# Two slot rings of an encoder trunk kernel: token-major evictions and Strassen weight loads drawn from other rings

## The chip, the cores and the metric

The kernel runs on one core of one Trainium2 chip. The metric is the device time of one execution in microseconds (us); lower is better. A time given for a kernel is the median of several executions; the profile and its trace come from one execution of their own. Engines are called by the profile's names: PE (matrix engine; PEld its weight loads), DVE (vector), ACT (scalar), POOL (GpSimd) and SP, whose queue issues nearly all DMAs.

## The reference

One layer (DEPTH is 1) over 512 tokens and 2048 channels, all float32. A conditioning vector gives six modulation vectors. A normed and modulated copy of x goes through one input projection whose columns feed four token mixers; their outputs are concatenated and projected back; then comes a gated convolutional feed-forward network of width 5504.

```
mod = cond @ ada_w[l] + ada_b[l]
h = rms_norm(x, mix_pre_g[l]) * (1.0 + sc_m) + sh_m
y = token_mixers(h, w_in[l], ...)            # DeltaNet | chunked attn | sliding window | gMLP, then @ w_out
x = x + gt_m * rms_norm(y, mix_post_g[l])
h = rms_norm(x, ffn_pre_g[l]) * (1.0 + sc_f) + sh_f
a, gt = split(h @ w_up, 2)
y = (gelu(causal_dwconv(a, conv_w) + conv_b) * gt) @ w_down
x = x + gt_f * rms_norm(y, ffn_post_g[l])
```

## The kernel before

**Matmuls.** Every large product is made from float32 operands that are split into a high and a low part; three matmuls of 128x128 by 128x512 stand for one. The split of a weight tile is one ACT copy (hi) and one DVE subtraction (lo); where it is "shadowed", ACT first copies the tile to PSUM as well (sh), and DVE subtracts that.

**Stages.** First the modulation vectors and the first input-projection groups ("early"), then the DeltaNet mixer with its long chain of small steps. The remaining ("late") input-projection groups bv, bk, ck, dv, bq, cq, du are written in the code after that chain, but the compiler that orders the queues mixes them into it: it lets each engine take what is ready, earlier lines of the code first. So PE fills the chain's pauses with late matmuls. Then come the other mixers, the output projection, and the feed-forward network. In that, three of 43 feature tiles are computed plainly (`up_plain`, PLAIN), the other 40 by a Strassen scheme: 20 blocks of the up projection (two passes `p` of ten) and 10 blocks of the down projection.

**Rings.** A tile with a tag takes one of the tag's `bufs` slots; a slot comes free when all readers of its former tile are done, and the slots of one tag go out in the order of the code. The rings that matter here:

- "t" in pool `tp`: NT_ = 3 slots of 128x512. It serves, among others, the evictions of the late groups: `ev_late_tm` (L762, token-major groups bv and dv, four evictions `lt` each, PSUM to SBUF by ACT, then a DMA to the DRAM buffer `std`) and `ev_late_fm` (`lf`).
- "xn" in pool `gp`: NBR = 5 slots. It holds the normed x while the early groups run; `rtile` draws from it for `bg_row`, `gate_row` and `ff_row`, whose rows are used from the output projection on.
- Three rings of four 128x1024 slots each for Strassen weights: `wraw` (pool `wp`, also the ring of all earlier weight loads, that of `up_plain` too), "raw1" (pool `ap`) and "raw2" (pool `dn`). `draw()` goes through them in a fixed order of twelve. A block (`fast_block`, L1449) draws eight, two for each of four j.

**The change of stage.** The activations h2 of the feed-forward network lie in pool `hp` as 16 hi and 16 lo tiles of 2 KB per partition (hl0 to hl15, then hh0 to hh15), 64 KB on the right-hand side. After the plain tiles `hold.close()` gives them up, and `dn` is opened there with waits tile by tile: its 46 KB (five t2, two ar, three hi and three lo, four raw2) lie on the last 46 KB of those 64, that is from hl9 on, with its tags in the order in which the code first asks for them: before, t2, ar, hi, lo, raw2. Just ahead of that, `late_sums` uses the four slots of "raw1" to load h2 blocks, form sums on DVE and store them to `h2d`.

**A block** has seven steps of 24 matmuls (X and Z are its PSUM banks). Step i needs A[i] (`a_tile`: load `ar`, hi on ACT, lo on DVE for even i and on POOL for odd) and one quarter of every weight pair; POOL makes the combined quarters T1 to T4 (L1468, L1471, L1473, L1475), of which T2 goes to a t2 tile and is used in step 2. In block 0, A[0] and A[1] are loaded ahead and A[2] to A[6] after steps 0 to 4.

**The tail.** After the last block, `wraw()` loads six units of plain down weights, and ten further `draw()` calls load gate rows and residual rows.

Of the kernel before, what the change touches and what calls it, by code (L numbers as in the profile page):

```python
# [10 lines left out]
F32 = mybir.dt.float32  # L11
# [5 lines left out]
P = 128  # L17
# [8 lines left out]
UW = 1024  # L26
# [223 lines left out]
def trunk_kernel(ctx: ExitStack, tc: tile.TileContext, a: dict, out: bass.AP):  # L250
# [26 lines left out]
    def nm(s):  # L277
        uid[0] += 1
        return f"{s}{uid[0]}"

    def mt(s="m", shape=(P, 512), dt=F32):
        return cur[0].tile(list(shape), dt, tag="m", name=nm(s))

    def tt_(s="t"):
        return tp.tile([P, 512], F32, tag="t", name=nm(s))
# [76 lines left out]
    def wraw():  # L362
        return wp.tile([P, UW], F32, tag="raw", name=nm("raw"), bufs=NRAW)
# [293 lines left out]
    for s, ks in enumerate(KSTEPS):  # L657
# [6 lines left out]
        for i, g in enumerate(gs):  # L664
# [6 lines left out]
            n = -(-len(fs) // max(1, len(gs) - 2 - i)) if s else FS0[i]  # L671
# [22 lines left out]
    def rtile(s, dt=F32):  # L694
        if mixing_open[0]:
            return gp.tile([P, 512], dt, tag="xn", name=nm(s), bufs=NBR)
        return mt(s, dt=dt)
# [62 lines left out]
        nc.sync.dma_start(out=std[STG[n_] + j], in_=t)  # L760

    def ev_late_tm(key, tt, ps, step):  # L762
        t = tt_("lt")
        S.activation(t, ps, AF.Gelu_apprx_tanh if key == "dv" else AF.Copy)  # L764
        nc.sync.dma_start(out=std[STG[key] + tt], in_=t)

    def late_groups(name, rate):
        pace[0] = rate
        for g in late:
            if (g[1][0][0] if g[0] == "FM" else g[1]) == name:  # L770
                if g[0] == "FM":
                    fm_group(g, ev_late_fm)
                else:
                    tm_group(g, ev_late_tm)

    def staged(name, j):
        t = mt("sd")
        nc.sync.dma_start(out=t, in_=std[STG[name] + j])
        return t
# [83 lines left out]
    for tt in range(NTT):  # L863
# [4 lines left out]
        t = mt("kp")  # L868
# [4 lines left out]
    for tt in range(NTT):  # L873
# [3 lines left out]
        t = mt("vt")  # L877
# [64 lines left out]
    for j in range(31):  # L942
        n = 31 - j
# [130 lines left out]
    for tt in range(NTT):  # L1074
        t = staged("dv", tt)
# [5 lines left out]
    for tt in range(NTT):  # L1081
        t = tmt[("dv", tt)]
        V.tensor_scalar(t, t, mv[:, tt, 0:1], vr[:, tt:tt + 1], ALU.subtract, ALU.mult)
        V.tensor_tensor(t, t, sgg, ALU.mult)
    for g in range(4):
# [4 lines left out]
        t = cur[0].tile([P, 512], F32, tag="sgo", name=nm("sgo"), bufs=4)  # L1090
# [7 lines left out]
    for h in range(H):  # L1098
# [18 lines left out]
        for j in range(NTT):  # L1117
# [3 lines left out]
            t = mt("pt")  # L1121
# [18 lines left out]
    for h in range(H):  # L1140
# [21 lines left out]
        for i0 in (0, 2):  # L1162
# [6 lines left out]
            t = mt("ct")  # L1169
# [235 lines left out]
    dn = [None]  # L1405
# [15 lines left out]
    def draw():  # L1421
        n = nraw[0] % (NRAW + NRAW1 + NRAW2)
        nraw[0] += 1
        if NRAW1 <= n < NRAW + NRAW1:
            return wraw()
        if n < NRAW1:
            return ap_[0].tile([P, UW], F32, tag="raw1", name=nm("raw"), bufs=NRAW1)
        return dn[0].tile([P, UW], F32, tag="raw2", name=nm("raw"), bufs=NRAW2)

    def t2(dt=F32):  # L1430
        return dn[0].tile([P, 512], dt, tag="t2", name=nm("t2"), bufs=NP + 1)
# [18 lines left out]
    def fast_block(A, src, units, bank, evict, after, own=False):  # L1450
        b = []
        for j in range(NP):
            d = {}
            for x, (k0, k1) in enumerate((("B11", "B12"), ("B22", "B21"))):
                raw = draw()
                nc.sync.dma_start(out=raw, in_=src[units[2 * j + x]])
                d[k0], d[k1] = raw[:, 0:512], raw[:, 512:]
            b.append(d)
# [153 lines left out]
    for ui, (uk, uc) in gdn[0]:  # L1612
        raw = wraw()
# [7 lines left out]
    for c in (0, 2):  # L1621
        t = draw()
        nc.sync.dma_start(out=t, in_=gtd[c:c + 2, :].rearrange("c n -> (c n)").partition_broadcast(P))
        gts.append(t)
    for tt in range(NTT):
        sl = slice(tt * P, (tt + 1) * P)
        sq = st(4)
        x1 = []
        for h in range(2):
            t = draw()  # L1630
            nc.sync.dma_start(out=t, in_=x1d[tt, h])
            x1.append(t)
        for cb in range(4):
            ps = mx("dl")
            for f in PLAIN:
                ah, al = acts[f]
                wh, wl = ws[(f, cb)]
                tm_mm(ps, ah[:, sl], al[:, sl], wh, wl, f == PLAIN[0], f == PLAIN[-1])
            y = ya[tt][cb]
            V.tensor_tensor(y, y, ps, ALU.add)  # L1640
            S.activation(t2(), y, AF.Square, accum_out=sq[:, cb:cb + 1])  # L1641
            G.tensor_tensor(y, y, gts[cb // 2][:, cb % 2 * 512:(cb % 2 + 1) * 512], ALU.mult)
        ss = st(1)
        V.reduce_sum(ss, sq, AX.X)
        r, _ = rstd(ss, D, "rf")
        for cb in range(4):
            y = ya[tt][cb]
            V.scalar_tensor_tensor(y, y, r, x1[cb // 2][:, cb % 2 * 512:(cb % 2 + 1) * 512], ALU.mult, ALU.add)  # L1648
            nc.sync.dma_start(out=out[sl, cb * 512:(cb + 1) * 512], in_=y)
# [6 lines left out]
NRAW = 4  # L1656
NHL = 5
NRAW1 = 4
NRAW2 = 4
# [29 lines left out]
```

## Time and profile before

| | |
|---|---|
| median of 3 runs | 2326.6 us (2317.59 to 2331.16) |
| profiled execution, its own time | 2319.29 us, of which the span is 2316.8 us |
| mean granted TensorE clock | 0.979 of full speed |
| PE busy | 2189.0 us, 94% of the span |
| DVE, ACT, POOL busy | 73%, 63%, 46% |
| DMA | 480.24 MB, mean 207 GB/s |

PE is busy in all but about 128 us of the span. Busy shares are averages over stages with different limits, so what a change in one place is worth is read from the idle time of PE in that place, and from what ended it. In the timeline a bracket behind an instruction gives the time for which its engine was idle before it, and the instruction or DMA that ended this wait.

### The profile page before, as it was taken

What the parts mean: (1) busy time and instruction counts of PE and PEld (TensorE: products, weight loads), DVE (VectorE), ACT (ScalarE), POOL (GpSimd) and SP (SyncE); (2) the same over time, 40 slices, a digit from 0 to 9 for tenths busy, and PEclk for the clock granted to TensorE, in tenths of its full rate; (3) what the DMA queues carried; (4) which work ended last, traced back from release to release, by engine and by line L of the source; (5) the groups of instructions that cost most, each with busy time, mean ns of one, the idle gap of its engine ahead of it and who ended that gap; (6) DMA issues with size and microseconds to landing.
All of it is one profiled execution on the core that took longest, in us unless ns stands there. A gap on an engine that the chain in (4) does not pass through costs nothing. (4 is left out here: it accounts for less than half of the span.)

```text
span 2316.8 us, 31339 instructions
## 1 busy us (share of the span) xinstructions
PE 2189.0 (94%) x9852; PEld 1734.0 (75%) x9852; DVE 1680.9 (73%) x2665; ACT 1463.4 (63%) x2638; POOL 1077.0 (46%) x848
## 2 busy tenths in 40 slices
PE   5999999989999998989999999999999999999998
PEld 3878876767677786767788887777777777877776
DVE  5887678877878545956665568788788767777777
ACT  5767465355567544666777677776776677666663
POOL 4663032243323200256445465755765765564643
PEclk8999999999999999999999999999999999999999
DMA  8876555677888754678853547456545634435333
GB/s 299 285 259 236 170 183 180 198 240 254 295 306 284 248 171 146 231 257 291 282 206 137 182 167 273 160 198 213 190 176 204 216 141 173 155 106 194 119 132 137
DMA packets 206574, 480.24 MB, mean 207 GB/s; under 512 B 32692, under 2 KB 74180, under 8 KB 206408
## 3 DMA queue, kind: packets, MB, share of 16 engines
q1 hardware_dynamic: 199576, 477.19, 59.1%
q10 hardware_dynamic: 6832, 1.06, 0.2%
q8 instruction: 78, 1.28, 0.2%
q14 instruction: 88, 0.72, 0.1%
HBM read 399.50 MB, written 78.67 MB: 206 GB/s over the span
## 5 line engine op out<-in xcount | busy, mean ns | idle before, releaser
L1481 PE MATMUL X<-hi,ah 128*128 128x512 f32 x960 | 386.8, 403 | 19.3 <-DVE c L1493 6.1
L435 POOL TENSOR_TENSOR ga<-ga,ada 128x512 f32<-128x512 f32 (+1 forms) x167 | 226.5, 1356 | 369.5 <-ACT ada L434 348.9
L1482 PE MATMUL X<-lo,ah 128*128 128x512 f32 x960 | 383.7, 400 | 1.0 <-DVE lo L1447 1.0
L1483 PE MATMUL X<-hi,al 128*128 128x512 f32 x960 | 383.4, 399 | 0.0
L1447 DVE TENSOR_TENSOR lo<-raw,hi 128x512 fp32r<-128x512 f32 x360 | 264.2, 764 | 110.7 <-ACT hi L1446 110.2
L1468 POOL TENSOR_TENSOR raw<-raw 128x512 f32<-128x512 f32 x120 | 161.9, 1353 | 319.3 <-ACT hi L1443 232.1
L1481 PE MATMUL Z<-hi,ah 128*128 128x512 f32 x720 | 286.8, 398 | 6.4 <-ACT c L1491 2.9
L1444 DVE TENSOR_TENSOR lo<-raw,sh 128x512 fp32r<-128x512 f32 x360 | 240.1, 683 | 72.2 <-ACT sh L1442 35.6
L1442 ACT ACTIVATE sh<-raw 128x512 fp32r<-128x512 f32 x360 | 210.5, 588 | 124.1 <-DMA raw<-w_dn 63.3
L1483 PE MATMUL Z<-hi,al 128*128 128x512 f32 x720 | 285.7, 397 | 0.8 <-POOL al L1418 0.8
L1482 PE MATMUL Z<-lo,ah 128*128 128x512 f32 x720 | 285.4, 396 | 0.0
L1446 ACT ACTIVATE hi<-raw 128x512 fp32r<-128x512 f32 x360 | 214.4, 625 | 95.2 <-PE X L1483 36.4
L1443 ACT ACTIVATE hi<-raw 128x512 fp32r<-128x512 f32 x360 | 221.4, 622 | 35.7 <-PE Z L1483 24.9
L1481 PEld LDWEIGHTS X<-hi,ah 128*128 128x128 f32 x960 | 183.1, 191 | 66.5 <-DVE c L1493 7.4
L380 PE MATMUL acc<-hh,hi 128*128 128x512 f32 x544 | 221.3, 410 | 9.2 <-ACT lt L764 6.7
L382 PE MATMUL acc<-hh,lo 128*128 128x512 f32 x544 | 221.5, 410 | 4.2 <-DVE lo L374 4.1
L381 PE MATMUL acc<-hl,hi 128*128 128x512 f32 x544 | 222.4, 409 | 0.4 <-POOL hl L493 0.3
L1482 PEld LDWEIGHTS X<-lo,ah 128*128 128x128 f32 x960 | 183.0, 191 | 43.2 <-DVE lo L1447 1.3
L1483 PEld LDWEIGHTS X<-hi,al 128*128 128x128 f32 x960 | 183.0, 191 | 42.7
L1481 PEld LDWEIGHTS Z<-hi,ah 128*128 128x128 f32 x720 | 135.7, 189 | 41.2 <-ACT c L1491 4.3
L432 DVE SCALAR_TENSOR_TENSOR ga<-ada,cond,ga 128x512 f32<-128x512 f32 (+1 forms) x183 | 148.7, 813 | 22.2 <-DMA ada<-ada 20.3
L376 ACT ACTIVATE hi<-raw 128x512 fp32r<-128x512 f32 (+1 forms) x162 | 97.6, 609 | 100.3 <-PE y L575 51.7
(363 smaller groups left out, 4698.0 us busy)
## 6 DMA issues: line engine op xcount, KB each, us to landing
ada<-ada SPq DMA_DIRECT2D x184, 512.0 KB, 4.6
raw<-w_up SPq DMA_DIRECT2D x172, 512.0 KB, 5.9
raw<-w_dn SPq DMA_DIRECT2D x86, 512.0 KB, 5.4
raw<-w_in SPq DMA_DIRECT2D x56, 512.0 KB, 4.4
partd<-c SPq DMA_DIRECT2D x80, 256.0 KB, 4.2
c<-partd SPq DMA_DIRECT2D x80, 256.0 KB, 3.7
actd<-q SPq DMA_DIRECT2D x40, 512.0 KB, 3.3
ar<-actd SPq DMA_DIRECT2D x35, 512.0 KB, 3.5
```

Source lines behind the costliest of these rows:

```text
L380: TE.matmul(o, sh, mh, start=first, stop=False)
L381: TE.matmul(o, sh, ml, start=False, stop=False)
L382: TE.matmul(o, sl, mh, start=False, stop=last)
L435: G.tensor_tensor(accs[eng], accs[eng], src, ALU.add)
L1442: S.activation(sh, src, AF.Copy)
L1443: S.activation(h_, src, AF.Copy)
L1444: V.tensor_tensor(l_, src, sh, ALU.subtract)
L1446: S.activation(h_, src, AF.Copy)
L1447: eng.tensor_tensor(l_, src, h_, ALU.subtract)
L1481: TE.matmul(ps, ah[:, sl], wh, start=st_, stop=False, skip_group_check=True)
L1482: TE.matmul(ps, ah[:, sl], wl, start=False, stop=False, skip_group_check=True)
L1483: TE.matmul(ps, al[:, sl], wh, start=False, stop=sp_, skip_group_check=True)
```

## The change

Two edits. `ev_late_tm` takes its tile from the five slots of "xn" (through `rtile`) in place of the three of "t". And `draw()` goes through its rings in another order: first the four of raw2, then raw1, then wraw, where it was raw1, wraw, raw2. As "raw2" is then the first tag of `dn` that the code asks for, it also becomes the first in that pool's layout. No instruction is added or removed.

```diff
     def ev_late_tm(key, tt, ps, step):
-        t = tt_("lt")
+        t = rtile("lt")
         S.activation(t, ps, AF.Gelu_apprx_tanh if key == "dv" else AF.Copy)
         nc.sync.dma_start(out=std[STG[key] + tt], in_=t)
...
     def draw():
         n = nraw[0] % (NRAW + NRAW1 + NRAW2)
         nraw[0] += 1
-        if NRAW1 <= n < NRAW + NRAW1:
-            return wraw()
-        if n < NRAW1:
+        if n < NRAW2:
+            return dn[0].tile([P, UW], F32, tag="raw2", name=nm("raw"), bufs=NRAW2)
+        if n < NRAW2 + NRAW1:
             return ap_[0].tile([P, UW], F32, tag="raw1", name=nm("raw"), bufs=NRAW1)
-        return dn[0].tile([P, UW], F32, tag="raw2", name=nm("raw"), bufs=NRAW2)
+        return wraw()
```

## Rows read from the trace of the kernel before

**Rows 1.** Page, part 1: busy us (share of the span) and instructions by engine.
```profile
PE 2189.0 (94%) x9852; PEld 1734.0 (75%) x9852; DVE 1680.9 (73%) x2665; ACT 1463.4 (63%) x2638; POOL 1077.0 (46%) x848
```
**Rows 2.** Windows: length, busy PE, PEld, DVE, ACT, POOL, clock, DMA share, GB/s.
```profile
999.00:1039.00 40.00, 32.50 (x123) 24.85 (x123) 21.80 (x30) 28.65 (x51) 30.03 (x24) 0.91 0.63 216
1160.00:1200.00 40.00, 40.00 (x173) 32.32 (x172) 24.18 (x37) 29.85 (x54) 20.20 (x16) 1.00 0.55 195
```
**Rows 3.** Timeline of ACT, evictions of bv: start, length, instruction, idle before.
```profile
316.69 2.00 ACT L764 ACTIVATE lt<-acc 128x512 f32<-128x512 f32 x3 [1.02 <-PE acc L575]
...
322.84 0.60 ACT L764 ACTIVATE lt<-acc 128x512 f32<-128x512 f32 x1 [3.36 <-DMA std<-lt]
...
326.14 0.63 ACT L843 ACTIVATE sq<-cv 128x512 f32<-128x512 f32 x1 [0.24 <-DVE cv L792]
```
**Rows 4.** Timeline of PE in the same place.
```profile
326.82 1.05 PE L846 MATMUL ss<-ones,sq 128*128 128x1 f32 x8 [2.21 <-ACT sq L843]
```
**Rows 5.** Timeline of ACT around the evictions of dv.
```profile
468.75 1.33 ACT L434 ACTIVATE ada<-ada,cond 128x512 f32<-128x512 f32 x2 [3.14 <-DMA ada<-ada]
...
478.56 0.60 ACT L764 ACTIVATE lt<-acc 128x512 f32<-128x512 f32 x1 [0.60 <-DMA std<-lt]
```
**Rows 6.** Timeline of PE in the same place.
```profile
472.56 0.80 PE L380 MATMUL acc<-hh,hi 128*128 128x512 f32 x1 [6.71 <-ACT lt L764]
```
**Rows 7.** By line and by tile: row loads and gate additions, first and last start.
```profile
L702 SPq DMA_DIRECT2D ga<-accd x16: 319/329/1537, 271.0 to 1375.8; - x16
...
L716 DVE TENSOR_TENSOR gt<-gt,gtps x8: 672/689/689, 753.6 to 1418.0; 128x512 f32<-128x512 f32 x8
```
**Rows 8.** Timeline of SP's queue around the first Strassen block.
```profile
985.71 2.65 SPq L1314 DMA_DIRECT2D h2d<-q  x3
988.41 5.89 SPq L1456 DMA_DIRECT2D raw<-w_up  x6
...
1002.82 0.33 SPq L1396 DMA_DIRECT2D pld<-fy  x1
1003.24 0.88 SPq L1416 DMA_DIRECT2D ar<-h2d  x2
...
1015.49 9.05 SPq L1416 DMA_DIRECT2D ar<-h2d  x2
```
**Rows 9.** Timeline of PE in the first Strassen block.
```profile
999.75 0.39 PE L1481 MATMUL X<-hi,ah 128*128 128x512 f32 x1
...
1005.33 0.39 PE L1481 MATMUL Z<-hi,ah 128*128 128x512 f32 x1
...
1015.54 0.50 PE L1481 MATMUL X<-hi,ah 128*128 128x512 f32 x1 [4.45 <-ACT hi L1443]
...
1016.66 0.63 PE L1481 MATMUL X<-hi,ah 128*128 128x512 f32 x1
...
1024.25 0.50 PE L1483 MATMUL Z<-hi,al 128*128 128x512 f32 x1 [0.84 <-POOL al L1418]
...
1030.84 0.50 PE L1481 MATMUL X<-hi,ah 128*128 128x512 f32 x1 [1.22 <-ACT hi L1446]
...
1032.34 0.50 PE L1482 MATMUL X<-lo,ah 128*128 128x512 f32 x1 [1.00 <-DVE lo L1447]
```
**Rows 10.** Timelines of ACT and POOL in the first Strassen block.
```profile
994.51 0.60 ACT L1442 ACTIVATE sh<-raw 128x512 fp32r<-128x512 f32 x1 [8.21 <-DMA raw<-w_up]
...
1011.97 0.60 ACT L1442 ACTIVATE sh<-t 128x512 fp32r<-128x512 f32 x1 [2.10 <-POOL t L1471]
...
1010.66 1.27 POOL L1471 TENSOR_TENSOR t<-raw,raw 128x512 f32<-128x512 f32 x1
```
**Rows 11.** By tile, raw: from issue to landing of its DMAs.
```profile
DMA to landing us min/median/max: 3.3/5.6/9.4
```
**Rows 12.** Timeline of ACT: last splits of plain down weights.
```profile
2267.34 1.15 ACT L376 ACTIVATE ah<-raw 128x512 fp32r<-128x512 f32 x2 [3.07 <-PE Z L1482]
...
2272.93 1.15 ACT L376 ACTIVATE ah<-raw 128x512 fp32r<-128x512 f32 x2 [4.43 <-PE X L1482]
```

## The prediction

> **What bounds the kernel.** The page's busy shares come first: PE works 2189.0 us, 94% [rows 1], so at most some 128 us lie in its pauses, and an edit that adds and removes no instruction can win or lose only there. The windows come second. In the middle of the Strassen blocks a window of 40 us has 40.00 us of PE at full clock; the window of the first block has 32.50 us and a granted clock of 0.91 [rows 2]. So the twelve slots of `draw` are no limit once the blocks run, and the order of three rings of equal size changes nothing there; only the entry into block 0 and the exit are left. The timelines come last, at the three places that the diff touches: the evictions of bv and dv (rows 3 to 7), the first block (rows 8 to 11) and the tail [rows 12].
>
> **Evictions, bv.** Three evictions of bv run at 316.69 without a wait; the fourth holds ACT idle for 3.36 us, until the store of the first has landed and its slot of three is free [rows 3]. ACT works in order: behind it stand the tanh and the square of the DeltaNet chain, whose square ends at 326.8, and PE waits 2.21 us for it [rows 4]. With five slots the fourth follows the third. The chain can come 3.36 us earlier; PE gains the 2.21 us for which it stood. Bounds: 0, if the next link is late by itself (DVE's part of the chain), to -3.4, if the chain leads PE further on. I take -2.2, the row that is PE's own.
>
> **Evictions, dv.** The fourth waits 0.60 us [rows 5], and no PE wait follows: 0. PE's 6.71 us there [rows 6] end with the first eviction, which needs no slot that is busy: ACT stands in L434, 3.14 us of it idle for a DMA, ahead of that eviction. A larger ring doesn't move it.
>
> **What the lt tiles take from "xn".** Slots of a tag go out in the order of the code, and the lt tiles stand ahead of `gate_row(8)`. That row was fetched from about 271 on; now it must wait until the dv tiles have their slots, near 478. It is first used at 753.6 [rows 7], so 270 us cover it: 0. If that cover were gone, a row would cost its three DMAs and a split, some 6 us by rows 11.
>
> **First weights of block 0.** Before, the first pairs took raw1 slots as soon as the `late_sums` stores had landed: issued from 988.41 [rows 8], split on ACT at 994.51 [rows 10], and step 0 started at 999.75 with no pause [rows 9]. Now they take raw2, which lies on hl9 to hl15 and hh0. These are read to the end of the plain tiles: the last 24 matmuls take channel tiles 8 to 15, three each, lo the second. Their pitch is that of step 0, (1005.33 - 999.75)/24 = 0.2325 us. So hl9 and hl10 are free near 996.2, hl14 near 999.0, hl15 near 999.7. From issue to landing is 3.3 (least) to 5.6 us (median) [rows 11]; sh and hi on ACT take 2 x 0.60. The first pair is ready at 996.2 + 4.5 to 6.8 = 1000.7 to 1003.0, the second (on hl13 and hl14) at 1003.5 to 1005.8; then three pairs of six matmuls, 4.2 us, end step 0 at 1007.7 to 1010.0 against 1005.33. That is +2.4 to +4.7; I take +3.5, the middle, as SP's queue is empty there. The other two pairs use raw1 and arrive as before.
>
> **The clock.** After the pause of 4.45 us seven matmuls last 0.63 against 0.39 (the one at 1016.66 stands for them), after the pause of 0.84 none does [rows 9]. So a slow stretch costs up to 7 x 0.24 = 1.7 us. A new pause of 1 to 3 us lies between: 0 to +1.7, I take +0.8. The Trainium skill (TensorE: Matmul & The Clock Gate, "HAM oscillation — how this bites in real kernels") says that a matmul stream interrupted by waits for DMA starts again at the lower clock each time; by it the term would be the full 1.7 and the forecast 0.9 us later. The trace agrees after the long pause only.
>
> **Step 2.** Before, its 4.45 us end the chain of T2: POOL's last T2 runs from 1010.66, ACT waits 2.10 us for it, then copies the two A tiles queued behind it and splits [rows 10]. T2 needs a t2 slot, and these lay on hl9 to hl13; behind raw2 they now lie on hh1 to hh5, free some 10 us before. T2 of the two late pairs needs weights landed by 999.7 + 5.6 = 1005.3, then four POOL steps of 1.3, then 1.2 of ACT: 1011.7, ahead of step 2's new turn at about 1014.4 (1008.8 + 5.6). So the 4.45 and their slow matmuls (1.7) go: -6.15. What is late next is A[2], loaded at 1003.24 behind the `pld` store and landed by about 1009 [rows 8, 11], still in time.
>
> **Steps 3 and 4.** 0.84 + 1.22 + 1.00 = 3.06 us of pauses [rows 9] and one more slow stretch of seven (1.7). They come from A[3] to A[5]: SP stands 9.05 us until the two ar slots are free [rows 8]. With ACT no longer held by T2 these slots are freed earlier, but the ar loads now queue behind four weight loads more. 0 to -4.8; I take -1.0, near the end that changes nothing, as POOL's share of the A tiles stays where it was.
>
> **Block 1, later blocks, tail.** Block 1 gets wraw, free since the plain splits, where it had raw2; the wait list shows no pause of PE at its start, so 0. In the tail the plain down weights wait for wraw slots of the last block's third and fourth pair instead of the first two, two pairs of splits (some 3 us) later. The last splits wait for PE in any case, 3.07 and 4.43 us [rows 12], which covers it: 0; without that cover +3 at most.
>
> **Sum.** Block 0: 3.5 + 0.8 - 6.15 - 1.0 = -2.85. With the bv evictions -5.05. The profiled execution took 2319.29 (span 2316.8 and 2.5 around it), 7.3 under the median of the three runs; the difference is applied to the median: 2326.6 - 5.05 = 2321.5. Ends: all at the good ends -3.4 + 2.4 - 6.15 - 4.8 = -12.0, 2314.6; all at the bad ends 4.7 + 1.7 - 6.15 = +0.3, 2326.9.
>
> **Rivals.** (1) *Slower: the store ahead of the weights.* SP issues in order. The `pld` store of the last plain tile went out only at 1002.82, though SP had nothing else from about 995 on, and the ar loads came behind it [rows 8]. It stands earlier in the code than the weights. If it is queued ahead of the raw2 loads, these go out from 1003.2 and land 3.3 to 5.6 later; step 0 starts at 1007.7 to 1010.0, +8 to +10.3. With the slow stretch (+1.7), less 6.15, less 2.2, that is +1.4 to +3.7: 2329. It decides from a start later than about 1006.4 (999.75 + 6.15 + 2.2 - 1.7). For it: the ar loads, which need hl15 too, came behind the store. Against: hl10 to hl14 are free before the store's data can be. The Trainium skill (DMA: Bandwidth & Descriptors, "Anatomy of one DMA — SWDGE (gpsimd) path") says that a DMA's semaphore wait is held on the issuing sequencer, not on the DMA engines; the trace agrees with SP's 9.05 us.
> (2) *Faster: the dv evictions move forward.* The queues are ordered anew, and a small shift could put the first dv eviction ahead of L434. PE's 6.71 would shrink to a table load and the eviction, 1.9, and the slow matmuls behind it (eight of 0.63, 1.9) would go: -6.7, 2314.8. For it: the order there hangs on a DMA that came late [rows 5]. Against: nothing in the change asks for it.
> (3) *No change: the losses only move.* PE's 2.21 is given back in the DVE-bound part of the chain that follows, and block 0 loses at its start what it saves at step 2: 2326. For it: step 0's terms add up to 4.3 of the 6.15 saved. Or the new order of the rings is taken up by the compiler with the same arrival times.
>
> **How the numbers follow.** Forecast 0.43, rival 1 0.17, rival 2 0.12, rival 3 0.23, other orders of the queues 0.05. The predicted time is 2321.5. The runs shown spread by 0.3% to each side, and 0.5% (11.6 us) is about what a measurement of this kernel can tell from no change. The range takes in rival 2 below and rival 1 with some of the spread above: 2313 to 2333. Faster by over 0.5% (under 2315.0): 0.06 of the forecast, 0.08 of rival 2, 0.02 others, 0.16. Slower by over 0.5% (over 2338.2): 0.04 of rival 1, 0.01 of rival 3, 0.03 others, 0.08. Within: 0.76.
>
> **What would show it.** The fourth bv eviction directly behind the third and no PE wait at L846 there; the first raw2 loads issued between 996 and 1000 (rival 1: behind the `pld` store); a pause of 1 to 3 us ahead of step 0 and none of over 1 us ahead of step 2; the 6.71 us still there (rival 2: gone). The prediction is wrong if PE's pauses outside these places differ by more than 10 us, as then the new order of the queues, and not the slots, sets the time.

## The result, and the profile after

| | before | after |
|---|---|---|
| median of 11 runs each, taken side by side | 2325.93 us | 2337.92 us (2331.16 to 2341.44) |
| ratio, with its 95% interval | | 1.0053 [1.004, 1.0066] |
| profiled execution: span, granted clock | 2316.8 us, 0.979 | 2329.2 us, 0.981 |

The change costs 12 us; the forecast was a gain of 5. The profiled execution of the kernel after is the fastest of its eleven. The page doesn't show the place: PE runs as many instructions as in [rows 1] and is busy 3.9 us less, so over the whole span all that was lost is idle time of PE, 144.1 us against 127.8.

```profile
PE 2185.1 (94%) x9852; PEld 1728.2 (74%) x9852; DVE 1686.6 (72%) x2665; ACT 1459.5 (63%) x2638; POOL 1083.6 (47%) x848
```

The places that the diff touches show it. Timelines of the kernel after, first the evictions of bv (ACT, PE), then PE at the first dv eviction, as in [rows 3, 4, 6]:

```profile
319.02 2.70 ACT L764 ACTIVATE lt<-acc 128x512 f32<-128x512 f32 x4 [1.04 <-PE acc L575]
327.86 1.05 PE L846 MATMUL ss<-ones,sq 128*128 128x1 f32 x8 [0.94 <-ACT sq L843]
471.78 0.79 PE L380 MATMUL acc<-hh,hi 128*128 128x512 f32 x1 [7.51 <-ACT lt L764]
```

The four evictions run back to back, PE's wait at L846 shrinks from 2.21 to 0.94, and the long wait at dv stays. That is as forecast. The first Strassen block isn't. SP, ACT and PE after, as in [rows 8 to 10]:

```profile
994.31 6.07 SPq L1456 DMA_DIRECT2D raw<-w_up  x6
1006.65 0.33 SPq L1396 DMA_DIRECT2D pld<-fy  x1
1007.07 1.84 SPq L1456 DMA_DIRECT2D raw<-w_up  x4
...
1020.46 0.33 SPq L1416 DMA_DIRECT2D ar<-h2d  x1
1040.50 0.33 SPq L1416 DMA_DIRECT2D ar<-h2d  x1
...
1011.29 0.60 ACT L1442 ACTIVATE sh<-raw 128x512 fp32r<-128x512 f32 x1 [7.96 <-DMA raw<-w_up]
1012.54 0.77 PE L1481 MATMUL X<-hi,ah 128*128 128x512 f32 x1 [6.70 <-POOL q L1313]
...
1040.52 0.79 PE L1483 MATMUL Z<-hi,al 128*128 128x512 f32 x1 [7.88 <-POOL al L1418]
```

The four raw2 loads, which step 0 needs first, go out at 1007.07, behind the `pld` store and behind six weight loads: some for the other two pairs, which come later in step 0, and some for block 1. PE stands 6.70 us ahead of step 0. (The releaser named is POOL, but it is the last event, not the cause: ACT's sh and hi of the first pair end at 1012.4.) Before, ACT had made that split at 994.51, five us before the plain tiles ended. Then a pause of 7.88 us stands ahead of step 3, where there had been 0.84. The block as a whole, from the start of step 0 to that of block 1, before and after (columns as in [rows 2]):

```profile
999.75:1050.50 50.75, 43.25 (x169) 33.53 (x168) 30.10 (x43) 36.48 (x64) 37.90 (x33) 0.93 0.69 238
```
```profile
1012.54:1069.73 57.19, 46.09 (x169) 35.41 (x169) 33.72 (x46) 38.73 (x69) 40.96 (x34) 0.84 0.66 229
```

It lasts 6.4 us longer: 3.6 more of idle PE and 2.8 more for the same 168 matmuls at a mean granted clock of 0.84. To compare executions whose earlier part differs by some us, all times of the Strassen part below are counted from the first plain matmul (L380, tile `up`): at 926.8 before, at 932.7 after. (Two of the expectations below put the start of block 1 a little late, at 137.5 and 140.3 for what is 137.1 and 139.9.)

| us from the first plain matmul | before | after | difference |
|---|---|---|---|
| start of step 0 of block 0 | 73.0 | 79.8 | +6.8 |
| start of block 1 | 123.7 | 137.0 | +13.3 |
| start of block 5 | 290.2 | 298.0 | +7.8 |
| last matmul | 1379.6 | 1385.6 | +6.0 |

So block 0 and its entry lose 13.3 us, blocks 1 to 4 give back 5.5, the later ones 1.8, and 6 stay. The other 5.9 us of the profiled executions arise ahead of the plain tiles.

### The profile page after: what moved, and what is told of

Its sections match the earlier page's. It is cut to its first block, busy times and chain, and to the rows that moved or that the text cites. A ratio compares the mean times of both kernels' runs of the same rounds, so it can differ in the third digit from the quotient of the medians.

```text
span 2329.2 us, 31291 instructions
## 1 busy us (share of the span) xinstructions
PE 2185.1 (94%) x9852; PEld 1728.2 (74%) x9852; DVE 1686.6 (72%) x2665; ACT 1459.5 (63%) x2638; POOL 1083.6 (47%) x848
## 3 DMA queue, kind: packets, MB, share of 16 engines
q8 instruction: 78, 1.28, 0.2%
## 5 line engine op out<-in xcount | busy, mean ns | idle before, releaser
L435 POOL TENSOR_TENSOR ga<-ga,ada 128x512 f32<-128x512 f32 (+1 forms) x167 | 232.1, 1390 | 393.4 <-ACT ada L434 367.1
L1447 DVE TENSOR_TENSOR lo<-raw,hi 128x512 fp32r<-128x512 f32 x360 | 270.8, 786 | 114.3 <-ACT hi L1446 113.7
L1444 DVE TENSOR_TENSOR lo<-raw,sh 128x512 fp32r<-128x512 f32 x360 | 240.3, 682 | 76.8 <-ACT sh L1442 42.9
L1481 PEld LDWEIGHTS X<-hi,ah 128*128 128x128 f32 x960 | 181.8, 190 | 69.9 <-DVE c L1493 10.4
L380 PE MATMUL acc<-hh,hi 128*128 128x512 f32 x544 | 221.8, 411 | 10.0 <-ACT lt L764 7.5
L377 DVE TENSOR_TENSOR lo<-raw,hi 128x512 fp32r<-128x512 f32 (+1 forms) x162 | 120.8, 759 | 65.1 <-ACT hi L376 63.7
L1483 PEld LDWEIGHTS Z<-hi,al 128*128 128x128 f32 x720 | 135.9, 189 | 39.7 <-POOL al L1418 8.2
```

The costliest lines, as they stand in the source:

```text
L380: TE.matmul(o, sh, mh, start=first, stop=False)
L435: G.tensor_tensor(accs[eng], accs[eng], src, ALU.add)
L1444: V.tensor_tensor(l_, src, sh, ALU.subtract)
L1447: eng.tensor_tensor(l_, src, h_, ALU.subtract)
L1481: TE.matmul(ps, ah[:, sl], wh, start=st_, stop=False, skip_group_check=True)
L1483: TE.matmul(ps, al[:, sl], wh, start=False, stop=sp_, skip_group_check=True)
```

## The experiments

Each stands with its edit, the expectation on record, and what came out. The median of the kernel before was 2323.7 to 2326.3 in these comparisons.

**The first edit alone**, with the old `draw`.

```
-        t = tt_("lt")
+        t = rtile("lt")
```

> The first edit alone: the lt evictions draw from the ring of five, draw keeps its old order. Theory 1 (two separate losses): the changed kernel enters the first Strassen block 5.9 us later than the kernel before, which is this edit's doing, because the gate rows come later in the code's order of slots and the queues are ordered anew from 580 us on; this kernel is then about 6 us slower than before, 2332, and its first Strassen matmul starts near 983. Theory 2 (all loss is the draw order's, the 5.9 us are the variation of one execution): 0 +- 2 us, 2326. Forecast on record for this edit: -2.2 us.

1.0011 [0.9996, 1.0027], 2330.2 against 2326.3: 2.6 us in the middle, and neither 0 nor 6 is excluded. So neither theory on record is decided. Its profiled execution reached the plain tiles at 939.0, so the time ahead of them varies by more than the 5.9 that I wanted to explain.

**The second edit alone**, with the old `lt`.

```
-        if NRAW1 <= n < NRAW + NRAW1:
-            return wraw()
-        if n < NRAW1:
+        if n < NRAW2:
+            return dn[0].tile([P, UW], F32, tag="raw2", name=nm("raw"), bufs=NRAW2)
+        if n < NRAW2 + NRAW1:
...
-        return dn[0].tile([P, UW], F32, tag="raw2", name=nm("raw"), bufs=NRAW2)
+        return wraw()
```

> The second edit alone: the new order of the rings, lt evictions as before. Theory 1 (two separate losses): about +6 us, 2332, with the start of the first block as in the changed kernel: weights issued behind the store of the last plain tile, some 6 us of PE pause ahead of step 0, a pause of some 8 us behind POOL's al later in the block. Theory 2 (all loss is here): +12 us, 2338. Theory 3 (all loss is the first edit's): 0. Forecast on record for this edit: -2.9 us; its slower rival: +3.6.

1.0038 [1.002, 1.0056], 2337.0 against 2326.3: 4.6 to 13 us slower, which leaves room for both of the first two theories and none for the third. Step 0 starts at 79.2, block 1 at 137.1, the last matmul at 1386.2, within 0.7 us of the changed kernel throughout. So block 0 is this edit's doing. Though nothing ahead of the plain tiles is changed here, they start at 934.3; in the 13 traces shown here that have no edit of the lt evictions they start between 924.5 and 935.7. The 5.9 us ahead of them can't be read from one pair of traces.

**The layout alone.** One unused tile makes raw2 the first tag of `dn`; the engines' queues hold the same instructions in the same order as before.

```
-    dn[0] = ctx.enter_context(pool("dn", 1, side="right", reuse_waits="tile"))
+    dn[0] = ctx.enter_context(pool("dn", 1, side="right", reuse_waits="tile")); dn[0].tile([P, UW], F32, tag="raw2", name=nm("raw"), bufs=NRAW2)
```

> The kernel before, but raw2 is the first tag that pool dn is asked for (one tile that nothing uses), so raw2 lies on hl9 to hh0 and t2 and ar behind it, as in the changed kernel, while draw keeps its old order. The queues hold the same instructions in the same order as before. Theory on record (step 2 waits for T2 because t2's slots come free late): the 4.45 us ahead of step 2 and their slow matmuls go, -6 us, 2320. Rival (POOL is late for another reason, such as its own queue): 0, 2326.

0.9989 [0.9969, 1.0009], step 0 at 73.8, block 1 at 124.8. PE and POOL in block 0:

```profile
1018.91 0.80 PE L1481 MATMUL X<-hi,ah 128*128 128x512 f32 x1 [4.43 <-ACT hi L1443]
1007.77 3.80 POOL L1471 TENSOR_TENSOR t<-raw,raw 128x512 f32<-128x512 f32 x3
1014.03 1.27 POOL L1471 TENSOR_TENSOR t<-raw,raw 128x512 f32<-128x512 f32 x1
```

The gap is 4.43 us, as before, though t2's slots are free sooner. The theory on record falls: T2 isn't late for want of a slot. The prediction's own dates say as much: hl9 to hl13 come free between about 996 and 999, and the last T2 ran from 1010.66. POOL's queue before shows why: from its first T1 on it works with one pause, of 0.49 us, and the last T2, that of [rows 10], is its twelfth instruction of some 1.3 us.

```profile
995.97 1.29 POOL L1468 TENSOR_TENSOR raw<-raw 128x512 f32<-128x512 f32 x1 [17.34 <-DVE lo L1444]
...
1004.39 3.80 POOL L1471 TENSOR_TENSOR t<-raw,raw 128x512 f32<-128x512 f32 x3
```

That T2 ends at 1011.93, 0.84 us into PE's pause. The other 3.6 us are ACT's, in the order of its queue. PE waits for the split of the first pair, whose T2 was long done; but this split stands behind the copy of the last T2 and behind two A tiles:

```profile
1012.98 1.99 ACT L1417 ACTIVATE ah<-ar 128x1024 fp32r<-128x1024 f32 x2
1014.88 2.18 ACT L1443 ACTIVATE hi<-t 128x512 fp32r<-128x512 f32 x4
```

So POOL's pace and ACT's order make the 4.45 us together. No run changed either of them alone, so the share of each is read from the trace and not shown.

**What delays step 0: four kernels.** All have the new `draw`. In two ACT issues the last plain tile's store; in two, four one-element copies on DVE keep block 1's first four loads back until the last raw2 tile of block 0 has landed.

```
-            nc.sync.dma_start(out=pld[f - PLAIN[0]], in_=y)
+            (nc.sync if first else nc.scalar).dma_start(out=pld[f - PLAIN[0]], in_=y)
```
```
-                raw = draw()
+                raw = draw(); 8 < nraw[0] < 13 and V.tensor_copy(raw[0:1, 0:1], held[0][0:1, 0:1])
...
-            b.append(d)
+            b.append(d); j == 1 and held.append(d["B22"])
```

> The second edit alone, and the store of the last plain tile (pld) is issued by ACT, which leaves it out of SP's queue; nothing else is moved. Theory a (the store that stands ahead of the raw2 loads in SP's queue delays step 0): the raw2 loads go out near 996 to 1000, step 0 starts at 1001 to 1003, and the kernel is 4 to 7 us faster than the one with the second edit alone. Theory b (POOL's order, with the sums of the second pass ahead of T1 and T2, sets the first block): step 0 starts earlier but the pauses behind it grow by as much, 0 to -2 us.

> The draw order alone with block 1's first four loads kept back, the pld store on SP's queue ahead of the raw2 loads as in the changed kernel. With the store on ACT as well, step 0 started 75.7 us after the first plain matmul; with neither or with the store on ACT alone 79.2 and 79.1. Theory (two limits that follow each other: the store holds the issue to about 74.5, and then the landing takes 3.3 us on free DMA engines): step 0 at 78 to 79. Rival (the loads for block 1 were the whole of it): 75.7.

> The draw order alone with the pld store on ACT's queue, and four one-element copies on DVE that keep block 1's first four wraw loads back until the last of the raw2 tiles of block 0 has landed. Times from the start of the first plain matmul to the start of step 0 and to the start of block 1: kernel before 73.0 and 123.7, draw order alone 79.2 and 137.5, with the pld store on ACT 79.1 and 140.3. Theory (the raw2 loads, issued 4 to 5 us sooner once the store is out of the way, landed 7.9 us later because the DMA engines were taken by loads for block 1): they now land in 3.5 to 5.6 us, step 0 starts at 74.5 to 76.5. Rival (the pause before step 0 isn't the loads'): 79. If POOL, which still has its sums first and works through the block without a pause, sets the end of the block, block 1 starts at 134 to 138 all the same.

| new draw with | raw2 loads from, first split at | step 0 | block 1 | ratio |
|---|---|---|---|---|
| nothing else | 74.3, 78.0 | 79.2 | 137.1 | 1.0038 [1.002, 1.0056] |
| store on ACT | 69.9, 77.8 | 79.1 | 139.9 | 1.0025 [1.0008, 1.0041] |
| loads held back | 74.4, 78.0 | 79.3 | 132.1 | 1.0019 [1.0004, 1.0034] |
| both | 69.5, 74.4 | 75.7 | 128.6 | 1.0002 [0.9987, 1.0016] |

SP and ACT with the store on ACT alone, then with both:

```profile
1002.24 4.79 SPq L1456 DMA_DIRECT2D raw<-w_up  x4
1010.11 0.60 ACT L1442 ACTIVATE sh<-raw 128x512 fp32r<-128x512 f32 x1 [6.65 <-DMA raw<-w_up]
```
```profile
1001.69 4.79 SPq L1456 DMA_DIRECT2D raw<-w_up  x4
1006.61 0.60 ACT L1442 ACTIVATE sh<-raw 128x512 fp32r<-128x512 f32 x1 [3.72 <-DVE fy L1371]
```

With the store out of the way the first of the loads goes out 4.4 us sooner, and the split starts no sooner: 7.9 us from the first issue to the split, against 4.9 or less where block 1's loads are held back. The windows from 994 to 1010 of the same two kernels show a reason, the DMA share (last column but one):

```profile
994.00:1010.00 16.00, 11.96 (x52) 9.27 (x50) 3.94 (x6) 1.42 (x2) 0.98 (x2) 1.00 1.03 371
```
```profile
994.00:1010.00 16.00, 13.55 (x55) 10.37 (x53) 3.95 (x6) 3.65 (x6) 4.67 (x6) 0.95 0.91 298
```

So there are two limits of almost the same height: the issue behind the store, and DMA engines full of loads that nobody needs yet. Taking away either alone leaves step 0 at 79; both together bring it to 75.7, in the range on record. (With the loads alone held back the range was 78 to 79, just missed.) With both, block 1 starts at 128.6, well ahead of the 134 to 138 that were on record in case POOL sets the end of the block, although its al still ends a pause of 6.49 us ahead of step 3. For the store alone neither theory on record fitted: step 0 didn't move, and block 1 started later, not sooner. The ratio of 1.0025 can't be told from 1.0038.

**Which rings come first.** Order raw1, raw2, wraw.

```
-        if n < NRAW2:
-            return dn[0].tile([P, UW], F32, tag="raw2", name=nm("raw"), bufs=NRAW2)
-        if n < NRAW2 + NRAW1:
-            return ap_[0].tile([P, UW], F32, tag="raw1", name=nm("raw"), bufs=NRAW1)
+        if n < NRAW1:
+            return ap_[0].tile([P, UW], F32, tag="raw1", name=nm("raw"), bufs=NRAW1)
+        if n < NRAW2 + NRAW1:
+            return dn[0].tile([P, UW], F32, tag="raw2", name=nm("raw"), bufs=NRAW2)
```

> Draw order raw1, raw2, wraw: block 0 takes its first two pairs from raw1 as in the kernel before and the other two from raw2; block 1 starts with wraw as in the changed kernel. Theory (what the change lost is the head start of POOL and ACT on the first two pairs): step 0 starts 73 us after the first plain matmul, as before; its third pair lands at 78 to 81, so one pause of 2 to 6 us inside step 0, and the whole is 0 to 4 us slower than before. Rival (block 1's loads that go ahead on the DMA engines are the cost): as slow as the draw order alone, +8.

1.0004 [0.9989, 1.0019]; step 0 at 73.5, block 1 at 122.5, with two pauses in step 0 (3.30 and 2.09) in place of the 4.45 of step 2. That fits the theory on record. The rival falls: block 1's loads go ahead of the raw2 loads here too. The cost of the new order was that the first pairs came from the ring that is free last.

**POOL relieved**, with the new draw, with the old one, and with each half of the relief alone on the old one.

```
-            (V, G)[i % 2].tensor_tensor(l_, raw, h_, ALU.subtract)
+            (V, G)[0 if early else i % 2].tensor_tensor(l_, raw, h_, ALU.subtract)
...
-                    A.append(a_tile(h2d[0], NA0 + i))
+                    A.append(a_tile(h2d[0], NA0 + i, True, True))
...
-            store = sums(G) if sums else None
+            store = sums(V) if sums else None
```

> The draw order alone, with POOL relieved in the first blocks: the sums of late_sums for the second pass and the lo parts of A[3] and A[5] of block 0 go to DVE (some 9 and 5 us of POOL's work in that block). Theory (POOL's work in block 0 starts only when the raw2 tiles land, 13 us later than in the kernel before, and POOL then is the bound: its al ends the 7.88 us of PE ahead of step 3): that pause falls below 2 us, block 1 starts 128 to 131 us after the first plain matmul against 137.5, and the kernel is 6 to 9 us faster than with the draw order alone, 2328 to 2331. Rival (the ar loads or the landings set the pause): 0 to -2 us.

0.9995 [0.9982, 1.0009]: 10 us below the draw order alone, where 6 to 9 were expected. The 7.88 us are gone, and block 1 starts at 127.7, at the edge of the 128 to 131 on record. One pause of 3.65 us, ended by DVE's lo, takes their place at step 2.

> The kernel before with the same relief of POOL. Theory (of the pauses in block 0 the 0.84, 1.22 and 1.00 us and one stretch of slow matmuls hang on the two ar slots, which POOL's al holds; the 4.45 us are POOL's own T2, behind eleven other T's since 996): the first go, the 4.45 stay, -3 to -5 us, 2321 to 2323. Rival (A[4] and A[5] land late for DMA reasons): 0.

0.9961 [0.9946, 0.9975], 2315.3 against 2323.7: faster than both kernels, and by more than expected. Block 1 starts at 120.4, 3.3 us sooner than before, and the last matmul 7.7 us sooner. So in this trace over half of the gain arises behind block 0; the sums that were moved stand in blocks 0 to 3. PE's only pause in block 0 that is left:

```profile
1022.66 0.79 PE L1481 MATMUL X<-hi,ah 128*128 128x512 f32 x1 [4.79 <-ACT hi L1443]
```

> The kernel before, only the lo parts of A[3] and A[5] of block 0 go to DVE; POOL keeps the sums. Theory (the ar slots, held by POOL's al, cause the 0.84, 1.22 and 1.00 us): block 1 starts 120 to 121 us after the first plain matmul against 123.7, and most of the gain of the full relief is here, 0.9965 to 0.998 of before. Rival (the sums are what holds POOL up): 123, 1.000.

> The kernel before, only the sums of late_sums for the second pass go to DVE; POOL keeps the lo parts. Theory (the sums stand behind T2 and T4 on POOL, only one set of them, 3 to 4 us, ahead of the al of A[3]): block 1 starts 122 to 124 us after the first plain matmul, 0.998 to 1.000 of before. Rival (the sums are the larger part of POOL's 14 us and carry the gain): 120 to 121, 0.9965.

With the lo parts alone block 1 starts at 118.8 (0.9997 [0.998, 1.0014]), with the sums alone at 119.5 (0.9976 [0.9962, 0.999]). In both traces all pauses of block 0 behind step 2 are gone, so either half is enough to let POOL catch up; neither theory on record foresaw that. Why the first isn't faster as a whole stays open: in its trace the 4.9 us won by block 1 are 2.4 at the last matmul.

**All of it together**, on the new draw and on the order raw1, raw2, wraw.

> The new draw order with all that was found to cost it taken away: the pld store on ACT's queue, block 1's first loads kept back, POOL's sums and the lo parts of A[3] and A[5] on DVE. Theory (these three are the whole of the loss, and the order itself brings nothing): as fast as the kernel before with POOL relieved, 0.996 of before, 2314 to 2318; block 1 starts 120 to 123 us after the first plain matmul, against 120.4. Rival 1 (the new order frees step 2 as forecast, once the rest is mended): 4 to 6 us faster than that. Rival 2 (something else of the order costs): 2320 or more.

> Order raw1, raw2, wraw with POOL relieved in the same way. Theory (the pauses of 3.30 and 2.09 us in step 0 stand for the 4.79 us ahead of step 2 in the kernel before with POOL relieved): the same time as that one, 0.996 of before. Rival (with raw1 first and T2 early on POOL, the relief finds more to remove): 0.993 to 0.995.

The first gave 1.0014 [0.9996, 1.0031], 2329.1, block 1 at 126.4: the theory fails, and the time is in the range of the second rival. One more cost inside block 0 is DVE's. Its queue around step 2, and PE's wait:

```profile
1026.36 1.41 DVE L1313 TENSOR_TENSOR q<-q 128x256 f32<-128x256 f32 x1
1027.69 2.31 DVE L1418 TENSOR_TENSOR al<-ar,ah 128x1024 fp32r<-128x1024 f32 x1
1029.92 1.27 DVE L1493 TENSOR_TENSOR c<-c,Z 128x512 f32<-128x512 f32 x2
1031.11 2.47 DVE L1444 TENSOR_TENSOR lo<-t,sh 128x512 fp32r<-128x512 f32 x4
...
1031.84 0.79 PE L1482 MATMUL X<-lo,ah 128*128 128x512 f32 x1 [3.15 <-DVE lo L1444]
```

The lo of T2, which PE waits for, stands behind the sums, al and two c's: the work taken from POOL now delays DVE. With the late first pairs all of it falls into the same 20 us; that this is why the relief fails here is my reading of the trace. Against it: the last matmul comes at 1379.9, no later than before (1379.6), and the interval overlaps those of the two reliefs taken singly. Why they don't add up stays open. The order raw1, raw2, wraw gave 0.9977 [0.996, 0.9995], with block 1 at 124.9 and 3.78 us for the same lo; the theory's 0.996 lies at the end of its interval, the rival's doesn't. The old draw order with POOL relieved has the lowest ratio of all, though the interval of this one overlaps its own.

**The halves of the first edit.** `rtile` for dv alone, and for bv alone.

```
-        t = tt_("lt")
+        t = rtile("lt") if key == "dv" else tt_("lt")
```

> The kernel before with the first edit for dv alone: only dv's lt tiles draw from the ring of five, so gate_row(8) still waits for them and its loads go from 271 us to behind 600. Theory 1 (the first edit costs a little, because the gate rows' loads and splits now fall into the stage from 600 to 770 us and the queues there are ordered anew): 2 to 4 us slower than before, the part from the first dv eviction to the first L1210 matmul lasts 300 to 306 us, where kernels without the edit took 296 to 301. Theory 2 (nothing of this shows; spread of executions): 0 +- 1.5 us, 296 to 301.

> The kernel before with the first edit for bv alone: gate_row(8) is fetched behind the bv evictions, near 330 us, and holds its slots from there. Theory 1 and the forecast on record for the bv evictions (PE's wait of 2.21 us at L846 falls to about 1, the stage from 600 to 770 stays as before): -1 to -2.2 us, 2324 to 2325. Theory 2 (what is won at bv is given back in the chain that follows): 0.

dv alone: 1.0028 [1.001, 1.0046], 306.5 us from the first dv eviction (with the table load ahead of it) to the first L1210 matmul. bv alone: 1.0008 [0.9992, 1.0025], 301.5 us. So a loss is clear of noise in dv's part alone, though the two intervals overlap; and the 1.0 to 1.3 us by which the wait at L846 shrinks in the three kernels with bv's edit can't be seen in the whole. (PE's queue as compiled is the same, line for line, for dv alone and for the whole first edit; the two ratios, 1.0028 and 1.0011, are to be read together.)

**The gate rows alone, late.** `lt` keeps its ring of three; beside each dv eviction a tile of "xn" is taken, and POOL writes one element of it.

```
-        t = tt_("lt")
+        t, x = tt_("lt"), (rtile("lx") if key == "dv" else None)
...
-        nc.sync.dma_start(out=std[STG[key] + tt], in_=t)
+        nc.sync.dma_start(out=std[STG[key] + tt], in_=t); x is not None and G.tensor_copy(x[0:1, 0:1], t[0:1, 0:1])
```

> The kernel before, with lt in the ring of three as ever; beside each of dv's evictions a tile of the ring of five is taken and one element copied to it on POOL, so that gate_row(8) is fetched as late as with the first edit (behind 600 us), while the evictions keep their own ring. Theory (the late gate rows alone are the first edit's cost): like the first edit for dv, 2 to 6 us slower than before, and 300 to 306 us from the first dv eviction to the first L1210 matmul. Rival (the cost is in the evictions' own new order and what the queues make of it, not in the gate rows): 0 +- 1.5 us, 296 to 301.

1.0021 [1.0007, 1.0035], 302.6 us: slower though the evictions keep their ring. Four one-element copies on POOL are the only work that was added. First row load in the kernel after and in this one, against 271.0 in [rows 7]:

```profile
L702 SPq DMA_DIRECT2D ga<-accd x16: 319/355/453, 666.7 to 1389.6; - x16
```
```profile
L702 SPq DMA_DIRECT2D ga<-accd x16: 319/336/1493, 669.4 to 1383.8; - x16
```

From the first L1107 matmul to the first L1210 matmul, the stage in which the rows are now fetched, the four kernels with late rows take 168.5 to 170.1 us (mean 169.4), the other fourteen traces, that of before among them, 162.9 to 168.1 (mean 164.7); the two ranges almost touch. The new pauses there end with DVE and ACT work of that stage, in the kernel after for instance these:

```profile
656.88 0.66 PE L1120 MATMUL pT<-cst,p 128*128 128x128 f32 x4 [2.69 <-DVE p L1063]
708.39 0.96 PE L573 MATMUL y<-hi,mh 128*128 128x512 f32 x3 [2.50 <-ACT hi L376]
757.38 0.44 PE L1168 MATMUL cT<-cst,cp 128*128 128x128 f32 x2 [3.06 <-DVE cp L1063]
```

The case for the late rows rests on the times, then, more than on this stage. Whether it is the rows' own loads and splits that are in the way, or the order that the compiler then gives to all the rest, these runs don't separate.

## Why the prediction was wrong

The step that failed is **step 2**, its -6.15. The pause of 4.45 us was taken for a wait for t2's slots. With the layout changed alone it stays (4.43); it comes from POOL's own pace, with a head start of 4 us on step 0 that isn't enough, and from ACT's order behind it. In the change that head start turns into a delay: POOL's first T1 comes at 1012.84, behind the start of step 0, and from there it works to 1043 without a pause. Step 2 has no pause any more, as forecast, but not for the reason given: counted from the first plain matmul PE comes to it 9 us later (93.5 against 84.3), and ACT now splits the first T2 at 1024.92, ahead of its copy of the last one at 1027.92. What was late next was not A[2], which I had checked, but A[3]'s lo on POOL, behind all the T's and four pieces of the sums (four more had run ahead of the first T1): 7.88 us, with eight slow matmuls behind it. From step 0 to block 1 the forecast had -6.15 and, for **steps 3 and 4**, -1.0; it was +6.4. I had the rows for it: POOL's L1471 in [rows 10] follows other work without idle time, and the 0.84 us in [rows 9] name POOL's al. POOL after:

```profile
1008.67 0.72 POOL L1310 TENSOR_TENSOR q<-q 128x256 f32<-128x256 f32 x1 [24.11 <-DMA q<-h2d]
...
1012.84 1.28 POOL L1468 TENSOR_TENSOR raw<-raw 128x512 f32<-128x512 f32 x1 [1.05 <-DMA raw<-w_up]
...
1038.13 2.34 POOL L1418 TENSOR_TENSOR al<-ar,ah 128x1024 fp32r<-128x1024 f32 x1
```

Point by point, the rest:

- **First weights, +3.5.** Measured +6.8 to step 0. The first slot is free when I said (with the store away, the first raw2 load starts at 1002.24, 3.7 us ahead of the end of the plain matmuls; I had 996.2 against 999.75). Two things were missed: the order in SP's queue, which I had as a rival only, and that the early loads of "the other two pairs" and of block 1 are not neutral. They take the DMA engines, and as ACT and POOL work in order, the pairs that land first can't be used first.
- **Rival 1** was right on the place and the side. Its start of step 0 (+8 to +10.3) was a little high, its 2329 far too low, since it still subtracted the 6.15. That the store alone decides is not so: with the store moved away step 0 starts as late.
- **The clock, +0.8.** After there are three stretches of matmuls of 0.63, behind the pauses of 6.70, 7.88 and one of 2.40 us at 1054.35, where before there were two. The kind was right; the size is in the 2.8 us above. After the 0.81 us at 1048.88 the granted clock stays at 1.00. The passage that I cited (Trainium skill, TensorE: Matmul & The Clock Gate, "HAM oscillation — how this bites in real kernels") has the trace on its side after these three pauses, but its example has longer waits than the 1 to 3 us that I applied it to.
- **The lt tiles and "xn", 0.** Wrong: the cover of 270 us was real for the row's arrival, but moving the gate rows alone cost 1.6 to 8.1 us (1.0021); that the stage where their work went had no room for it is the likely reason, and is not shown. I had priced when the row is needed and not what stands where it goes.
- **Evictions of bv, -2.2.** The mechanism held, PE's own wait gave 1.27 of the 2.21, and nothing of it is seen in the time. **Evictions of dv, 0:** right, 7.51 us are still there, so rival 2 didn't happen.
- **Block 1 and later, 0.** Blocks 1 to 4 give 5.5 us back. Part of it is in their pauses: 6.6 us ended by ACT's c (L1491) in blocks 1 to 3 before, 3.3 after. Rival 3's kind of shift, then, but on the side of the loss. **Tail, 0:** the last Strassen matmul and the last matmul of all lie 33.7 us apart before and 33.6 after.

## What to carry to other kernels

Where engines that work in order feed a stage, give the buffers that come free first to the work that is used first; here a ring that was free early but used late only filled the DMA engines. Before a gap is put down to a slot, look whether the engine behind it was idle: if it worked without a pause, a slot that comes free sooner won't help, and less work ahead or an earlier start is what to try. Then follow the gap through the next engine's queue, which may hold back work that is long ready. And a tile that moves to another ring moves every later user of that ring; price those where they land, not where they are due.

## What the runs showed of the hardware

In these runs an addition or subtraction on DVE with both operands in SBUF took up to 3.6 times as long beside POOL. With all reliefs on the new draw order, DVE's addition L1310 took 0.42 us at 1010.56, while POOL stood still, and 1.51 us at 1021.91, beside POOL's L1473, which itself took 2.28 where a T alone takes 1.28. The subtraction L1418 took 1.21 us at 1033.51, just ahead of POOL's next instruction (1033.56), and 2.31 at 1027.69, just behind one (1027.45).

```profile
1010.56 0.42 DVE L1310 TENSOR_TENSOR q<-q 128x256 f32<-128x256 f32 x1
...
1018.75 0.69 DVE L1444 TENSOR_TENSOR lo<-raw,sh 128x512 fp32r<-128x512 f32 x1 [0.27 <-ACT sh L1442]
...
1021.91 1.51 DVE L1310 TENSOR_TENSOR q<-q 128x256 f32<-128x256 f32 x1
...
1033.51 1.21 DVE L1418 TENSOR_TENSOR al<-ar,ah 128x1024 fp32r<-128x1024 f32 x1
...
1013.19 1.28 POOL L1468 TENSOR_TENSOR raw<-raw 128x512 f32<-128x512 f32 x1 [24.62 <-DVE lo L1444]
...
1020.86 2.28 POOL L1473 TENSOR_TENSOR raw<-raw,raw 128x512 f32<-128x512 f32 x1
...
1027.45 1.47 POOL L1471 TENSOR_TENSOR t<-raw,raw 128x512 f32<-128x512 f32 x1
...
1033.56 3.53 POOL L1475 TENSOR_TENSOR raw<-raw,t 128x512 f32<-128x512 f32 x2
```

L1444, whose second operand is the PSUM copy sh, takes 0.68 to 0.69 with POOL at work and without. The Trainium skill (SBUF — State Buffer, "SBUF: two separate sides") says that a DVE operation with two SBUF inputs and a GpSimd operation that reads SBUF exclude each other, and that the one that starts first holds the ports for its whole length; these rows agree. So the time of such an instruction, moved from POOL to DVE, is not to be taken from a stretch in which the other engine was idle.
